# Decoder step on one core: other pacing of the mixer's convolution and LayerNorm, the last convolution tap stored to SBUF directly, sample caches read in pairs, and a different share of weights split by DMA

## Chip, core and metric

The kernel runs on one core of one Trainium2 chip. The metric is the device time of one execution in microseconds (us), from the first to the last activity of the run; less is better.

## What is computed

One inference step of a two-layer decoder over 320 tokens: 256 of a new prompt and 64 of a sample group (8 sequences of 8 tokens) that has cached state. Both groups use the same weights. Cut to what matters here, a layer is

```
x += 1/2 * SwiGLU_1(RMSNorm(x))
h  = RMSNorm(x);  u, v, q, g = split(h @ W_in)
A  = pool_mixer(u) @ w_pool * scale          # 4 groups, trailing windows 2, 4, 8, 16
z  = v_a * sigmoid(v_gate)                   # GLU
y  = causal depthwise convolution of z, 31 taps, + bias
B  = silu(LayerNorm over the 1024 channels of y) @ W_pw
C  = attention of q over 256 memory rows     # keys, values: projected (prompt) or cached (sample)
x += (sig(g_A)*A + sig(g_B)*B + sig(g_C)*C) @ W_out
x += 1/2 * SwiGLU_2(RMSNorm(x))
```

with d_model 1024, 4 heads and d_ff 2816, all in fp32. The new states, the projected keys and values and the final RMSNorm are outputs as well.

## The kernel before

Activations lie transposed: 8 blocks of 128 channels by 320 token columns. Every weight block of 128x128 fp32 numbers is split into a high part `whi` and a low part `wlo`, and each product is three matmuls of 320 columns: high by high (L309), high by low (L310), low by high (L312). A **unit** is 8 such blocks, 24 matmuls, and the text counts units from the start of the layer: the first FFN has units 0 to 65, the memory keys 66 to 73, the GLU 74 to 89, the memory values 90 to 97, q 98 to 105, the four pool groups (each with its gate g_A) to about 123, g_C to about 131, g_B to 139, then W_pw, W_out and the second FFN. Layer 1 repeats this 222 units later.

`Stream` brings the weights. Raw tiles of 1 MB (two units each, four buffers) come over SP's queue in the fixed order of `stream_plan`, which also sets where the cached keys ("k") and values ("v") of the sample group stand among them. `Stream.split` prepares a unit three units ahead of its use: ScalarE (ACT) casts the raw block to `whi` (L235) and VectorE (DVE) subtracts to get `wlo`. While `ws.share` is set, every third unit goes another way: ACT casts (L228), then writes the negative of the raw block, rounded, into `wlo` (L229), and GpSimd (POOL) issues an accumulating DMA (L230, `wlo<-in_w`) that adds the raw weights to it from HBM. There are four `whi` and four `wlo` buffers. `ws.share` is set through the whole mixer.

All arithmetic of DVE and POOL goes through a helper, so those instructions have line L127. Beside the matmuls the mixer runs small generators, stepped once per weight unit or so by `pump` at a rate that `start` gives them: `conv_gen` (rate RC) runs two lanes of the depthwise convolution, one channel block each, where ACT makes the first tap in PSUM (L503), DVE adds 30 taps there (`cv<-z,cst,cv`), and ACT copies the sum to SBUF (L510, `z<-cv`); `conv_sample` (rate RS) does the 64 sample columns on POOL (tile `pr`), and ACT adds the bias (L538). When all blocks are there, DVE sums them to `ysum`, a matmul with a matrix of ones gives the mean (L357), DVE subtracts it, ACT squares, a second such matmul gives the variance, DVE forms the reciprocal root, and after the gate "open" ACT applies silu (L585) and the cast to `chi` (L586), which W_pw multiplies. `pool_gen` (rate RP) makes the pooled inputs `plh` and `pll` from `ut`, which ACT fills from PSUM (L770). `prompt_scores` has the softmax of the prompt, with exponentials on ACT (L601). `sample_scores` and `sample_values` multiply the cached raw tiles.

Each engine runs its own queue in order. The rates only set where the program text issues a step; the order in each queue is then set by the tile framework's scheduler from its own estimate of times.

Of the kernel before, what the change touches and what calls it, by code (L numbers as in the profile page):

```python
# [17 lines left out]
TP = 256  # L18
# [14 lines left out]
LA = 3  # L33
NBIG = 8
C_LEAD = 24
RC = 2.5
RS = 1.0
RP = 2

C_G1, C_GM, C_G2, C_GK, C_PS, C_BD, C_LG, C_LB, C_WD = 0, 8, 16, 24, 32, 40, 48, 56, 64  # L40
# [11 lines left out]
def stream_plan():  # L52


    at = {}
    seq = []
    nb = 0
    for l in range(L):
        c = l * LP
        seq += list(range(c, c + MP))  # L60
        seq += list(range(c + MP + 8, c + MP + 12))
        seq += list(range(c + MP, c + MP + 8))
        seq += list(range(c + MP + 12, c + LP))
        at.setdefault((nb + NJ * 16) // 16, []).append(("m", l))
        nb += NJ * 24
        nb += 128 + 64 + 64 + 64
        for g in range(4):
            nb += 16 + (4 if g else 0)
            at.setdefault((nb + C_LEAD) // 16, []).append(("k", l, 2 * g))
            nb += 16  # L70
            at.setdefault((nb + C_LEAD) // 16, []).append(("k", l, 2 * g + 1))
        for b in range(8):
            nb += 8
            at.setdefault((nb + C_LEAD) // 16, []).append(("v", l, b))
            if b == 1:
                nb += 4
        nb += 64 + 64 + 64
        nb += NJ * 24
    assert seq and nb == 16 * len(seq) and sorted(seq) == list(range(nb // 16))
    items = []  # L80
    for n, c in enumerate(seq):
        items += at.get(n, [])
        items.append(("w", c))
    return items, seq
# [3 lines left out]
def trunk_kernel(  # L88
# [49 lines left out]
    def bigt(shape, dt, s):  # L138
        return big.tile([P] + shape, dt, name=nm(s), tag="big")
# [29 lines left out]
    def ccol(l, off, i):  # L169
        c = l * C_LAYER + off + i  # L170
        return cst[:, c:c + 1]
# [4 lines left out]
    class Stream:  # L176
# [45 lines left out]
        def split(self, u):  # L222
            c, half = seq[u // 2], u % 2
            raw = self.piece("w", c)[:, half * 1024:half * 1024 + 1024]
            hi = wp.tile([P, 1024], F32R, name=nm("whi"), tag="whi")
            lo = wp.tile([P, 1024], F32R, name=nm("wlo"), tag="wlo")
            if self.share and u % 3 == 2:
                nc.scalar.copy(hi[:, :], raw)  # L228
                nc.scalar.mul(lo[:, :], raw, -1.0)  # L229
                nc.gpsimd.dma_start(lo[:, :], w_in[c][:, half * 1024:half * 1024 + 1024], accum_op=ALU.add)  # L230
            else:
                n = 512 if u == 0 else 1024
                for e in range(0, 1024, n):
                    h, r = hi[:, e:e + n], raw[:, e:e + n]
                    nc.scalar.copy(h, r)  # L235
                    dve.tensor_tensor(out=lo[:, e:e + n], in0=r, in1=h.bitcast(F32), op=ALU.subtract)
            self.units[u] = (hi, lo)
            if half == 1:
                self.done("w", c)
# [256 lines left out]
    def conv_lane(l, z, y, blocks, zdone, cdone):  # L496

        for j in blocks:
            while j not in zdone:
                yield  # L500
            zt = z[j // 4][:, j % 4, :]
            acc = psum("cv", 2)
            nc.scalar.activation(acc[:, :TP], zt[:, 0:TP], AF.Identity, bias=ccol(l, C_BD, j), scale=ccol(l, C_WD, j))  # L503
            yield
            yield
            for k in range(1, TAPS):
                dve.scalar_tensor_tensor(out=acc[:, :TP], in0=zt[:, k:k + TP], scalar=ccol(l, C_WD, k * 8 + j),
                                               in1=acc[:, :TP], op0=ALU.mult, op1=ALU.add)
                yield
            nc.scalar.copy(y[j][:, :TP], acc[:, :TP])  # L510
            cdone.append(j)

    def conv_sample(l, z, y, zdone, cdone, sdone):

        for j in range(KB):
            while j not in zdone:
                yield
            zt = z[j // 4][:, j % 4, CB + TP:ZW]
            pr = tp.tile([P, 1280], F32, name=nm("pr"), tag="pr", bufs=1)
            pr = pr[:, :16 * TS].rearrange("p (k t) -> p k t", t=TS)  # L520
            for half in range(2):
                n = 16 - half
                v = zt[:, half * 16 * 8:half * 16 * 8 + 1]
                win = bass.AP(v.tensor, v.offset, [list(v.ap[0]), [8, n], [1, TS]])
                w = ccol(l, C_WD, (CB - 16 * half) * 8 + j)
                wv = bass.AP(w.tensor, w.offset, [list(w.ap[0]), [-8, n], [0, TS]])
                if half == 1:
                    pool.tensor_copy(pr[:, 15, :], pr[:, 0, :])
                pool.tensor_tensor(out=pr[:, 0:n, :], in0=win, in1=wv, op=ALU.mult)
                m = 8  # L530
                while m:
                    pool.tensor_tensor(out=pr[:, 0:m, :], in0=pr[:, 0:m, :], in1=pr[:, m:2 * m, :], op=ALU.add)
                    m //= 2
                yield
            yield
            while j not in cdone:
                yield
            nc.scalar.activation(y[j][:, TP:T], pr[:, 0, :], AF.Identity, bias=ccol(l, C_BD, j))  # L538
            sdone.append(j)

    def conv_gen(l, z, zdone, ch, gate):
# [35 lines left out]
            yield  # L577
        while "open" not in gate:
            yield
        ch.append((bigt([KB, T], F32R, "chi"), bigt([KB, T], F32R, "clo")))  # L580
        hi, lo = ch[0]
        for j in range(KB):
# [99 lines left out]
    def mixer(l, mh, acc, on_block):  # L682
# [13 lines left out]
                dve.tensor_tensor(out=lo[:, k, :], in0=hf[:, :], in1=hi[:, k, :].bitcast(F32), op=ALU.subtract)  # L696
                yield

        ws.share = True
        wide[0] = 0  # L700
        defer(lambda: start("norm", norm_gen(), 4), 2)
        kv_keys(l, mh)
# [3 lines left out]
        for i in range(2):  # L706
            pool.memset(z[i][:, :, 0:CB], 0.0)
            nc.gpsimd.dma_start(z[i][:, :, CB + T:ZW], sc_in[l, :, 4 * i:4 * i + 4, :])
        ch, gate, zdone = [], [], []
        for j in range(KB):  # L710
            pa = pwide() if j < 2 else pmm()
            chain(pa[:, :T], xs, T)
# [11 lines left out]
                    start("conv", conv_gen(l, z, zdone, ch, gate), RC)  # L724

            defer(zfin)
        va = bigt([2048 + KB * TS], F32, "va")
        vt = va[:, :2048].rearrange("p (b c) -> p b c", b=2)
        sgs = va[:, 2048:].rearrange("p (k t) -> p k t", k=KB)
# [5 lines left out]
        ats = qa[:, KB * TP:].rearrange("p (k t) -> p k t", k=KB)  # L735
        qz = bigt([2, 1056], F32, "qz")
        pool.memset(qz[:, :, :], 0.0)
        for o in range(KB):
            pq = pmm()
            chain(pq[:, :T], xs, T)  # L740
# [21 lines left out]
        for g in range(4):  # L762
# [43 lines left out]
            start("pool", pool_gen(), RP)  # L806
            if g % 2 == 0:
                sc = psum("sa", 1)
            sample_scores(l, qz, sc, 2 * g)
            for i in range(2):  # L810
                pg = pmm()
                chain(pg[:, :T], xs, T)
                nc.scalar.activation(merged[:, 2 * g + i, :], pg[:, :T], AF.Sigmoid)
            sample_scores(l, qz, sc, 2 * g + 1)
            drain("att")
            if g % 2 == 1:
# [2 lines left out]
                pps.append(pp)  # L819
                start("ss", sample_softmax(sc, pp), 1)  # L820

        po = None
        for o in range(KB):
            pc = pmm()
# [20 lines left out]
            if o % 4 == 0:  # L845
                drain("so")
                po = psum("sa", 1)
            sample_values(l, pps[o // 4], po, o)
            if o % 4 == 3:
                start("so", sample_out(po, ats, o // 4), 1)  # L850
        sgb = bigt([KB, T], F32, "sgb")
# [9 lines left out]
        while "conv" in side:  # L861
            for name in ("convs", "conv"):
                if name in side and next(side[name][0], "end") == "end":
                    side.pop(name, None)
        ws.share = False
        chi, clo = ch[0]
        mg = (bigt([KB, T], F32R, "mgh"), bigt([KB, T], F32R, "mgl"))
        cx = [(chi[:, k, :], clo[:, k, :]) for k in range(KB)]
# [188 lines left out]
```

## Time and profile before

| | us |
|---|---|
| runs | 1683.77, 1684.36, 1684.89 |
| median | 1684.36 |
| profiled execution, its own time | 1683.86 |
| its span, first to last instruction | 1682.1 |
| PE busy, of the span | 1640.5 (98%) |
| DVE busy | 1122.7 (67%) |
| ACT busy | 796.4 (47%) |
| POOL busy | 278.3 (17%) |
| mean granted clock of TensorE | 0.991 |

TensorE (PE) is busy nearly always, so the time is the number of matmuls plus what PE waits. The waits are read from the waits and the timeline of PE; the stages in which another engine is full are read from the windows, where a busy time near the window's length means that the engine has nothing to spare there. The units are placed in the trace by counting the weight loads.

### The profile page before, as it was taken

Reading aid. Unit: us, or ns where it says so; the run is one execution under the profiler, and the core shown is the slowest. Engines: PE = TensorE matmul, PEld = TensorE weight load, DVE = VectorE, ACT = ScalarE, POOL = GpSimd, SP = SyncE. Lnnn points to the kernel's source line nnn. Section 1 sums busy time; section 2 is a strip of 40 time slices with the busy share of each in tenths; the row PEclk is TensorE's granted clock in tenths of the full one; section 3 lists DMA queues with packets and bytes.
Section 4 is the critical chain, followed back from the end, with each engine's and each line's share of the span. In section 5 each row is a group of like instructions: output and inputs, shape, how many; then the busy total and the mean of one; then the engine's idle time right before and its main releaser. Section 6 shows DMA issues by size and latency. Waiting matters only on the chain.

```text
span 1682.1 us, 27304 instructions
## 1 busy us (share of the span) xinstructions
PE 1640.5 (98%) x11194; PEld 1590.9 (95%) x11194; DVE 1122.7 (67%) x1832; ACT 796.4 (47%) x1201; POOL 278.3 (17%) x298
## 2 busy tenths in 40 slices
PE   8999999999999999999999999999999999999996
PEld 8999999988888999999999999998988889999996
DVE  7555648999945676555465564689999367655544
ACT  5444535456645454443344443454657364444431
POOL 2000004586510000000000000047664000000000
PEclk9999999999999999999999999999999999999998
DMA  7444448786897344444444444587778954444430
GB/s 272 151 150 151 176 149 261 217 250 189 267 309 237 125 151 151 151 150 151 151 150 151 151 151 170 187 256 213 215 233 262 316 171 151 151 150 151 150 126 32
DMA packets 48189, 308.87 MB, mean 184 GB/s; under 512 B 5824, under 2 KB 5888, under 8 KB 14912
## 3 DMA queue, kind: packets, MB, share of 16 engines
q1 hardware_dynamic: 38160, 270.75, 45.1%
q0 software_dynamic: 9616, 36.05, 10.1%
q8 instruction: 88, 1.44, 0.3%
q10 hardware_dynamic: 288, 0.33, 0.1%
q14 instruction: 37, 0.30, 0.1%
HBM read 298.28 MB, written 8.82 MB: 183 GB/s over the span
## 4 chain that ended last, share of the span: by engine, by line
PE 84%; DVE 10%; POOL 2%; ACT 1%; DMA 1%; issue 1%; DVEq 0%; SPq 0%; POOLq 0%; ACTq 0%
PE mm L309 19%; PE mm L310 19%; PE mm L312 19%; PE cv L310 8%; PE cv L309 8%; PE cv L312 8%; DVE cv L127 4%; DVE wlo L127 2%; POOL pr L127 2%; DVE us L127 1%; PE sa L664 1%; DMA wlo<-in_w 1%; PE st L833 1%; DVE ysum L127 0%; DVE pll L127 0%
## 5 line engine op out<-in xcount | busy, mean ns | idle before, releaser
L235 ACT CAST whi<-raw 128x1024 fp32r<-128x1024 f32 (+1 forms) x397 | 414.8, 1045 | 438.7 <-PE mm L310 255.9
L127 DVE TENSOR_TENSOR wlo<-raw,whi 128x1024 fp32r<-128x1024 f32 (+1 forms) x397 | 502.1, 1265 | 176.9 <-PE mm L312 70.0
L309 PE MATMUL mm<-hhi,whi 128*128 128x320 f32 x1712 | 512.5, 313 | 6.6 <-ACT hhi L361 5.8
L310 PE MATMUL mm<-hlo,whi 128*128 128x320 f32 x1712 | 509.0, 311 | 0.0
L309 PEld LDWEIGHTS mm<-hhi,whi 128*128 128x128 f32 x1712 | 321.8, 188 | 18.7 <-ACT hhi L361 6.2
L310 PEld LDWEIGHTS mm<-hlo,whi 128*128 128x128 f32 x1712 | 322.1, 188 | 1.4 <-issue 0.4
L312 PE MATMUL mm<-hhi,wlo 128*128 128x320 f32 x1712 | 288.4, 309 | 0.0
L312 PEld LDWEIGHTS mm<-hhi,wlo 128*128 128x128 f32 x1712 | 260.5, 188 | 0.3
L127 DVE SCALAR_TENSOR_TENSOR cv<-z,cst,cv 128x256 f32<-128x256 f32 x480 | 204.6, 478 | 3.7 <-ACT cv L503 2.0
L230 POOL DMA_DIRECT2D wlo<-in_w x48 | 42.7, 889 | 984.2 <-ACT wlo L229 637.7
L310 PE MATMUL cv<-hlo,whi 128*128 128x320 f32 x592 | 175.4, 310 | 0.0
L309 PE MATMUL cv<-hhi,whi 128*128 128x320 f32 x592 | 174.2, 309 | 0.0
L127 POOL TENSOR_TENSOR pr<-pr 128x512 f32<-128x512 f32 (+3 forms) x128 | 124.6, 973 | 7.7
L309 PE MATMUL mm<-hidh,whi 128*128 128x320 f32 x418 | 123.8, 309 | 0.0
L310 PE MATMUL mm<-hidl,whi 128*128 128x320 f32 x418 | 123.7, 309 | 0.0
L365 ACT CAST hidh<-up 128x320 fp32r<-128x320 f32 x88 | 40.0, 459 | 159.5 <-DVE up L127 159.5
L310 PEld LDWEIGHTS cv<-hlo,whi 128*128 128x128 f32 x592 | 111.2, 188 | 0.2
L309 PEld LDWEIGHTS cv<-hhi,whi 128*128 128x128 f32 x592 | 110.9, 188 | 0.0
L312 PE MATMUL cv<-hhi,wlo 128*128 128x320 f32 x592 | 98.8, 309 | 0.0
L312 PEld LDWEIGHTS cv<-hhi,wlo 128*128 128x128 f32 x592 | 89.9, 188 | 0.2
L127 DVE TENSOR_TENSOR up<-mm,rstd 128x320 f32<-128x320 f32 x53 | 26.0, 490 | 88.2 <-PE mm L312 88.2
L309 PE MATMUL cv<-hidh,whi 128*128 128x320 f32 x286 | 84.7, 309 | 0.0
(196 smaller groups left out, 2324.7 us busy)
## 6 DMA issues: line engine op xcount, KB each, us to landing
raw<-in_w SPq DMA_DIRECT2D x221, 1024.0 KB, 4.8
wlo<-in_w POOLq DMA_DIRECT2D x48, 512.0 KB, 7.8
raw<-in_kc SPq DMA_DIRECT2D x16, 1024.0 KB, 7.5
raw<-in_vc SPq DMA_DIRECT2D x16, 1024.0 KB, 7.5
out_co<-z POOLq DMA_DIRECT2D x16, 135.0 KB, 5.1
raw<-in_mem SPq DMA_DIRECT2D x2, 1024.0 KB, 4.8
out_mk<-kt POOLq DMA_DIRECT2D x2, 1024.0 KB, 10.2
out_mv<-va POOLq DMA_DIRECT2D x2, 1024.0 KB, 5.2
```

Of the source, the lines that this page charges most:

```text
L127: return op(*args, **kw)
L230: nc.gpsimd.dma_start(lo[:, :], w_in[c][:, half * 1024:half * 1024 + 1024], accum_op=ALU.add)
L235: nc.scalar.copy(h, r)
L309: nc.tensor.matmul(out, hi, xh, start=(i + e == 0), stop=False)
L310: nc.tensor.matmul(out, hi, xl, start=False, stop=False)
L312: nc.tensor.matmul(out, lo, xh, start=False, stop=(i + e == last))
L365: nc.scalar.copy(hi, src)
L664: nc.tensor.matmul(po[32 * h:32 * h + 32, :256], pp[:, at:at + 32], raw[:, mb * 1024 + h * 256:mb * 1024 + h * 256 + 256], start=(bb == 0 ...
L833: nc.tensor.matmul(pv[:, :TP], vt[:, mb, o * P:o * P + P], kt[:, 2 * hd + mb, :], start=(mb == 0), stop=(mb == 1))
```

## The change

- Pacing: RC goes from 2.5 to 3, RS from 1 to 2 with two more stopping points in each block's work, and once the gate is open the rate of the convolution's generator, which by then does the last part of LayerNorm, is set to a new RN of 6.
- The first convolution tap moves from ACT to DVE (a `tensor_scalar` into PSUM); the last of the 30 additions writes the SBUF tile itself, so that ACT's copy L510 is gone.
- The sample caches are read in pairs: both key tiles of a group behind its two g_A blocks, before one ahead of them and one behind; value tiles two at every second g_C block. `stream_plan` places the tiles accordingly.
- `ws.share` takes every second unit, not every third, but is set only in the GLU stage and from q to the end of the pool groups of each layer: four stages in all. Since a split runs three units ahead, these are units 78 to 92 and 102 to 126 of a layer.

The counts of instructions that differ: the accumulating DMAs and ACT's negations 48 to 42, DVE's subtractions `wlo` 395 to 401; ACT's first taps and copies 16 and 16 to none; DVE gets 16 `tensor_scalar`; ACT's table loads 26 to 30. The number of matmuls is the same.

```diff
@@ constants
-RC = 2.5
-RS = 1.0
+RC = 3.0
+RN = 6.0
+RS = 2.0
@@ stream_plan
         for g in range(4):
-            nb += 16 + (4 if g else 0)
-            at.setdefault((nb + C_LEAD) // 16, []).append(("k", l, 2 * g))
-            nb += 16
-            at.setdefault((nb + C_LEAD) // 16, []).append(("k", l, 2 * g + 1))
-        for b in range(8):
-            nb += 8
-            at.setdefault((nb + C_LEAD) // 16, []).append(("v", l, b))
-            if b == 1:
-                nb += 4
+            nb += 32 + (4 if g else 0)
+            at.setdefault((nb + C_LEAD) // 16, []).extend([("k", l, 2 * g), ("k", l, 2 * g + 1)])
+        for b in range(1, 8, 2):
+            nb += 16 + (4 if b == 1 else 0)
+            at.setdefault((nb + C_LEAD) // 16, []).extend([("v", l, b - 1), ("v", l, b)])
@@ Stream.split
-            if self.share and u % 3 == 2:
+            if self.share and u % 2 == 0:
@@ conv_lane
-            nc.scalar.activation(acc[:, :TP], zt[:, 0:TP], AF.Identity, bias=ccol(l, C_BD, j), scale=ccol(l, C_WD, j))
-            yield
+            dve.tensor_scalar(out=acc[:, :TP], in0=zt[:, 0:TP], scalar1=ccol(l, C_WD, j), scalar2=ccol(l, C_BD, j),
+                              op0=ALU.mult, op1=ALU.add)
             yield
             for k in range(1, TAPS):
-                dve.scalar_tensor_tensor(out=acc[:, :TP], in0=zt[:, k:k + TP], scalar=ccol(l, C_WD, k * 8 + j),
+                dst = acc[:, :TP] if k < TAPS - 1 else y[j][:, :TP]
+                dve.scalar_tensor_tensor(out=dst, in0=zt[:, k:k + TP], scalar=ccol(l, C_WD, k * 8 + j),
                                                in1=acc[:, :TP], op0=ALU.mult, op1=ALU.add)
                 yield
-            nc.scalar.copy(y[j][:, :TP], acc[:, :TP])
             cdone.append(j)
@@ conv_sample
                 pool.tensor_tensor(out=pr[:, 0:n, :], in0=win, in1=wv, op=ALU.mult)
+                yield
                 m = 8
                 while m:
                     pool.tensor_tensor(out=pr[:, 0:m, :], in0=pr[:, 0:m, :], in1=pr[:, m:2 * m, :], op=ALU.add)
                     m //= 2
+                    if m == 4:
+                        yield
                 yield
@@ conv_gen
         while "open" not in gate:
             yield
+        side["conv"][1] = RN
@@ mixer
-        ws.share = True
         kv_keys(l, mh)
...
+        ws.share = True
         for j in range(KB):          # GLU
...
+        ws.share = False
         kv_values(l, mh, vt)
...
+        ws.share = True
         for o in range(KB):          # q
...
-            sample_scores(l, qz, sc, 2 * g)
             for i in range(2):
                 pg = pmm()
                 chain(pg[:, :T], xs, T)
                 nc.scalar.activation(merged[:, 2 * g + i, :], pg[:, :T], AF.Sigmoid)
+            sample_scores(l, qz, sc, 2 * g)
             sample_scores(l, qz, sc, 2 * g + 1)
...
+        ws.share = False
         for o in range(KB):          # g_C
...
-            sample_values(l, pps[o // 4], po, o)
+            if o % 2 == 1:
+                sample_values(l, pps[o // 4], po, o - 1)
+                sample_values(l, pps[o // 4], po, o)
...
-        ws.share = False
         chi, clo = ch[0]
```

The queues' order changes in three places that the prediction speaks of. The first is PE's queue around the matmul that gives LayerNorm's mean (`ysum`, the sum of the eight blocks; `hhi` and `hlo` are the normalised input, `mm`, `cv` and `st` PSUM tiles). Before, in layer 0, it stands behind unit 133, in the g_B stage:

```order
L309 MATMUL mm_5323<-hhi_2483,whi_5185 128x320
L310 MATMUL mm_5323<-hlo_2484,whi_5185 128x320
L312 MATMUL mm_5323<-hhi_2483,wlo_5186 128x320 x8
L357 MATMUL cv_5377<-ysum_2809,ones 128x320
L309 MATMUL mm_5361<-hhi_2483,whi_5236 128x320
```

In the changed kernel it stands inside unit 125, in g_C's first blocks (`st<-kt,va` is attention of the prompt):

```order
L306 MATMUL mm_4935<-hhi_2483,whi_4760 128x320
L307 MATMUL mm_4935<-hlo_2484,whi_4760 128x320
L354 MATMUL cv_4815<-ysum_2807,ones 128x320
...
L309 MATMUL mm_4935<-hhi_2483,wlo_4761 128x320 x4
L837 MATMUL st_4978<-kt,va_3351 128x256 x2
```

It moved ahead by eight units of weights, and the variance's matmul, which follows it, stands in unit 127 and no longer in 137. In layer 1 the mean's matmul stands one unit earlier still, in 124 by the same count. W_pw begins at unit 140 in both.

The second is ACT's queue in pool group 1 of layer 0, between the copy of the transposed scores `kt` and the copies to `ut`. Before:

```order
L229 ACTIVATE wlo_4086<-raw_3872 128x1024
L630 COPY kt<-st_4075 128x512
L510 COPY z_2732<-cv_3920 128x256
L235 CAST whi_4127<-raw_3978 128x1024
L601 ACT_TABLE_LOAD
L601 ACTIVATE ex_4137,sm_4139<-st_4096,mx_4138 128x256 x2
L503 ACTIVATE cv_4622<-z_2732,cst 128x256
L770 COPY ut_4081<-mm_4084 128x320
```

Changed:

```order
L804 CAST plh_4027<-us_4032 128x640
L815 ACTIVATE merged_3908<-mm_4062 128x320
L538 ACTIVATE z_2730<-pr_3711,cst 128x64
L631 COPY kt<-st_4125 128x512
L225 CAST whi_4178<-raw_4011 128x1024
L602 ACT_TABLE_LOAD
L602 ACTIVATE ex_4189,sm_4191<-st_4147,mx_4190 128x256 x2
L773 COPY ut_4131<-mm_4134 128x320
L226 ACTIVATE wlo_4179<-raw_4011 128x1024
```

The copy `z<-cv`, which waits for DVE's taps, and the first tap `cv<-z,cst` are gone from between them; the accumulated exponentials now follow a cast and a table load directly, and a negation `wlo<-raw` stands behind the first copy to `ut`.

The third is POOL's queue around the last sample block of the convolution in layer 0. Before:

```order
L127 TENSOR_TENSOR pr_5020<-z_2732,cst 128x1024
...
L127 COPY pr_5020<-pr_5020 128x64
L127 TENSOR_TENSOR pr_5020<-z_2732,cst 128x960
L771 DMA out_po<-ut_4564 128x2x135
L127 TENSOR_TENSOR pr_5020<-pr_5020 128x512
L127 TENSOR_TENSOR pr_5020<-pr_5020 128x256
L127 TENSOR_TENSOR pr_5020<-pr_5020 128x128
L127 TENSOR_TENSOR pr_5020<-pr_5020 128x64
L230 DMA wlo_4722<-in_w 128x1024
L127 MEMSET ut_12289 128x2x15
L765 DMA ut_12289<-in_sp 128x2x120
L127 MEMSET qz_3540 128x1056
```

Changed:

```order
L124 COPY pr_4511<-pr_4511 128x64
L124 TENSOR_TENSOR pr_4511<-z_2730,cst 128x960
L124 TENSOR_TENSOR pr_4511<-pr_4511 128x512
L124 MEMSET ut_12328 128x2x15
L768 DMA ut_12328<-in_sp 128x2x120
L124 TENSOR_TENSOR pr_4511<-pr_4511 128x256
L227 DMA wlo_4803<-in_w 128x1024
L124 TENSOR_TENSOR pr_4511<-pr_4511 128x128
L124 MEMSET qz_3572 128x1056
L124 TENSOR_TENSOR pr_4511<-pr_4511 128x64
```

The fill of `ut`, the load of its sample columns, one accumulating DMA and the fill of `qz` stood behind the block's last addition and now stand among its additions, ahead of the last one.

## Rows read from the trace of the kernel before

**Rows 1.** The page, part 1: busy us, share of the span, instructions.

```profile
PE 1640.5 (98%) x11194; PEld 1590.9 (95%) x11194; DVE 1122.7 (67%) x1832; ACT 796.4 (47%) x1201; POOL 278.3 (17%) x298
```

**Rows 2.** The page, part 4: the chain that ended last, by engine.

```profile
PE 84%; DVE 10%; POOL 2%; ACT 1%; DMA 1%; issue 1%; DVEq 0%; SPq 0%; POOLq 0%; ACTq 0%
```

**Rows 3.** Windows of the mixer: us, engines' busy us (instructions), granted clock, DMA share, GB/s.

```profile
310.00:350.00 40.00, 36.99 (x203) 33.08 (x203) 39.58 (x71) 20.55 (x27) 31.30 (x30) 1.00 0.76 211
350.00:395.00 45.00, 45.00 (x309) 43.78 (x308) 44.08 (x84) 30.14 (x62) 31.62 (x30) 1.00 0.77 223
395.00:450.00 55.00, 51.57 (x363) 44.63 (x362) 53.95 (x107) 32.44 (x55) 29.00 (x34) 0.97 0.76 246
...
1225.00:1280.00 55.00, 51.66 (x364) 44.70 (x363) 53.95 (x107) 32.96 (x56) 28.16 (x33) 0.97 0.75 243
```

**Rows 4.** Waits of PE: engine line waited for, us in total, times, longest us.

```profile
PE mm L309 <- ACT chi L586: 7.9, 2, 3.9
PE mm L309 <- ACT ut L770: 7.3, 5, 3.0
PE mm L490 <- DMA wlo<-in_w: 6.3, 2, 3.2
```

**Rows 5.** Windows, five short stretches, columns as above.

```profile
411.56:414.97 3.41, 3.41 (x16) 1.88 (x16) 3.41 (x5) 2.10 (x5) 3.21 (x2) 0.50 0.00 0
548.10:554.90 6.80, 6.20 (x23) 6.20 (x24) 3.97 (x9) 5.79 (x14) 0.00 (x0) 0.50 0.47 157
1172.73:1176.14 3.41, 3.41 (x10) 2.64 (x9) 3.22 (x7) 0.00 (x0) 1.51 (x3) 0.50 0.78 191
1241.00:1244.40 3.40, 3.40 (x18) 1.78 (x17) 3.40 (x5) 1.69 (x4) 3.32 (x3) 0.50 0.00 0
1377.53:1380.94 3.41, 3.41 (x14) 3.41 (x14) 1.49 (x4) 3.41 (x9) 0.00 (x0) 0.50 0.67 279
```

**Rows 6.** Timeline of PE: start us, us, instruction; inside unit 125, mean's matmul.

```profile
476.46 0.31 PE L309 MATMUL mm<-hhi,whi 128*128 128x320 f32 x1
...
522.41 0.70 PE L357 MATMUL cv<-ysum,ones 128*128 128x320 f32 x2
```

**Rows 7.** Timeline of ACT, layer 0: a copy and what follows it.

```profile
406.90 0.38 ACT L510 COPY z<-cv 128x256 f32<-128x256 f32 x1 [5.01 <-DVE cv L127]
...
408.24 1.28 ACT L601 ACT_TABLE_LOAD   x1
...
410.94 0.43 ACT L770 COPY ut<-mm 128x320 f32<-128x320 f32 x1
```

**Rows 8.** Timeline of POOL, layer 0: the issue for the unit that PE waits for.

```profile
337.19 0.89 POOL L230 DMA_DIRECT2D wlo<-in_w  x1 [0.18 <-issue]
```

**Rows 9.** One line (L230) of 270 to 560: DMA landings.

```profile
DMA to landing us min/median/max: 5.2/7.9/11.3
```

**Rows 10.** Groups by line, 279 to 459: busy us, mean ns, idle before.

```profile
L127 DVE SCALAR_TENSOR_TENSOR cv<-z,cst,cv 128x256 f32<-128x256 f32 x240 | 102.2, 477 | 1.9 <-ACT cv L503 1.0
...
L127 DVE TENSOR_TENSOR wlo<-raw,whi 128x1024 fp32r<-128x1024 f32 x30 | 46.5, 1549 | 0.5 <-PE mm L312 0.3
...
L229 ACT ACTIVATE wlo<-raw 128x1024 fp32r<-128x1024 f32 x15 | 15.9, 1060 | 0.1
...
L503 ACT ACTIVATE cv<-z,cst 128x256 f32<-128x256 f32 x8 | 4.5, 568 | 2.7 <-DVE z L127 2.6
...
L510 ACT COPY z<-cv 128x256 f32<-128x256 f32 x8 | 3.0, 372 | 7.6 <-DVE cv L127 7.5
```

**Rows 11.** Timeline of POOL, layer 0: the last sample block.

```profile
450.44 1.97 POOL L127 TENSOR_TENSOR pr<-z,cst 128x1024 f32<-128x1024 f32 x1
...
464.26 0.92 POOL L230 DMA_DIRECT2D wlo<-in_w  x1
...
469.21 1.00 POOL L127 MEMSET qz<- 128x1056 f32 x1
```

**Rows 12.** Timeline of DVE, layer 0: the last addition to ysum.

```profile
466.60 0.49 DVE L127 TENSOR_TENSOR ysum<-ysum,z 128x320 f32<-128x320 f32 x1
```


## The prediction

> **What bounds the kernel now.** I read the page's engine shares first, then the chain, then the windows over the mixer, then PE's waits. PE is busy 1640.5 of 1682.1 us [rows 1] and holds 84% of the chain that ended last; DVE holds 10% of it [rows 2]. So a microsecond is gained only where PE stands still or runs at half clock, or where matmuls go, and no matmul goes here. The windows show a second limit: from 310 to 450 us, the stretch with the depthwise convolution, DVE is busy 39.58 of 40, 44.08 of 45 and 53.95 of 55 us, and in layer 1 again 53.95 of 55 [rows 3]. DVE is full there while PE still has a little idle time. A PE wait in that stretch can only be handed back as far as DVE keeps up.
>
> PE's waits that the change touches come in three kinds, each once per layer [rows 4]: for `chi`, LayerNorm's last product (7.9 us together); for the copy to `ut` (7.3 us in five waits, of which two long ones of about 3.0); and for an accumulating DMA in the memory values (6.3 us). Five stretches of half clock (0.50, the 1.2 GHz level) follow waits of some 3 to 4 us [rows 5]: one after each `chi` wait, one after each `ut` wait, one after the DMA wait of layer 1. They cost half their length where PE had work: 3.1 us of the stretch at 548.10 (6.20 busy), 1.7 of each 3.41.
>
> **The change, part by part.**
>
> *LayerNorm earlier.* The mean's matmul ran at 522.41 us and would now stand in unit 125, a place that PE passed at 476.46 [rows 6]; the variance follows two units behind and not four. In the new order the last casts of `chi` stand in unit 134, six units ahead of W_pw, and a unit lasts 24 x 0.147 = 3.5 us, so there are some 20 us of cover. Even 10 us of lateness leaves `chi` in time. The two waits go with their half clock: 7.9 + 3.1 + 1.7 = **12.7 us** [rows 4, 5].
>
> *Unit 95 is no longer shared.* Its DMA was issued only at 337.19 [rows 8], because POOL stood in the sample block. DVE now makes this `wlo`. The two waits go, with layer 1's half clock: 6.3 + 1.7 = **8.0 us** [rows 4, 5]. Units 90 and 92 remain shared; unit 92's place in PE's queue is the same as before, so I cost it at nothing, covered by the landing that was in time before.
>
> *ACT's copies go.* At 406.90 ACT had waited 5.01 us for DVE's taps in order to copy them; the table load, exponentials and the copy to `ut` at 410.94 stood behind it [rows 7], and PE waited for `ut`. In the new queue nothing of the taps stands there. Two waits of 3.0 with two half-clock stretches: 6.0 + 3.4 = **9.4 us** [rows 4, 5]. Next in line there is DVE (the pooled inputs). The four additional table loads take 1.28 us each, like the one from 408.24 to 409.53 [rows 7]; ACT is busy 20.55 of 40 and 32.44 of 55 us [rows 3], so its idle time hides them.
>
> If nothing came back, that would be 12.7 + 8.0 + 9.4 = 30.1 us.
>
> *What DVE must do.* Between the last z (330 us) and the last tap, by my count of the queue, DVE has 26 subtractions where it had 29, and eight first taps more. Three subtractions at 46.5/30 = 1.55 us are 4.6 us less. The first tap as a `tensor_scalar` into PSUM has no row: below it is bounded by a later tap, 102.2/240 = 0.43 us, above by ACT's 0.57 for the same work [rows 10]; I take 0.43, the same engine and shape, and get 3.4 us more (at most 4.6). So DVE's load is about 1 us smaller per layer (0 to 2): **practically unchanged**. The last tap's store to SBUF I cost at nothing, below at nothing and above at 0.1 us each, as its neighbours are of equal length; 16 are 1.6 us. DVE therefore cannot finish the taps 8 us earlier, though PE could. The generous pacing also changes the mixture: in the new queue more taps of the first six blocks stand behind subtractions and pooled sums, and block 6 ends, by adding the rows' durations along the queue, some 4 us later than before.
>
> *LayerNorm's first wait.* The mean needs `ysum`, whose last addition ran at 466.60 [rows 12], after POOL's last block, which took from 450.44 to 464.26 [rows 11], 13.8 us. In the new queue an accumulating DMA's issue (0.92), the fill of `qz` (1.00) and the fill and load of `ut` (I take 0.9 for both, as for the other issue) stand inside that block [rows 11]: 2.8 us more. With block 6 later by 4, `ysum` is done near 466.6 + 0.5 + 2.8 + 4 = 474 us of the old time scale. PE would be there at 476.46 less the 3.2 of unit 95 and 4.7 of `ut`, at about 468.6. In a queue in order it waits: about 5 us. Layer 1 has the mean's matmul one unit earlier but had 1.7 us more to give; I take 5 there too. **Given back: 10 us** of the 17.4; from 2 (DVE and POOL overlap better than added up) to 17.4 (all of it).
>
> *New sharing in the GLU stage.* Every second unit now needs an accumulating DMA. For most of them PE has 14.1 us of matmuls between the release of the buffer and the need (96 of 0.147), and the path is a cast of 1.05, a negation of 1.06 [rows 10], 0.3 to the issue and 7.9 to landing [rows 9], 10.3 in sum: covered, and the slowest landing of 11.3 still is, nearly. Unit 78 has only 53 matmuls, 7.8 us, since units 74 to 77 run interleaved. It is late by 2.5 us at the median landing; by 0 at the fastest (5.2) and 5.9 at the slowest. I take 2.2, as PE has small delays there too: **4.4 us more** for both layers, range 0 to 12.
>
> The Trainium skill, page "DMA: Bandwidth & Descriptors", section "Anatomy of one DMA", fits a GpSimd-issued DMA by 2.0 us plus its bytes at 436 GB/s, which for 512 KB would be an estimate of 3.2 us. By that rule unit 78 would be in time and the sum 4.4 us lower. The trace does not agree: of 22 landings none was under 5.2 us [rows 9].
>
> *Caches in pairs.* The same 32 tiles and matmuls in another order; they land ahead of use by several us before. Nothing, with an upper bound of 1 us per pair at four value pairs of each layer: 0 to 8. The six fewer accumulating DMAs lie in stages that were not late, apart from unit 95.
>
> **Sum**: -12.7 - 8.0 - 9.4 + 10 + 4.4 = -15.7 us. The profiled execution took 1683.86 us, 1.8 more than its span and 0.5 less than the median of the runs; from it, 1668.2: I forecast **1668 us**. Own range: 1660 (2 given back, unit 78 in time) to 1676 (nearly all given back).
>
> **The rivals.**
> *All waits vanish (B).* DVE's queue and POOL's fit after all and the DMAs land: 1683.9 - 30.1 = 1654. For it: DVE loses its dependence on ACT at both ends of a block, with 5.0 us waits of ACT on it. Against: DVE is 98% busy [rows 3]. Chance 0.12.
> *Only `chi` remains (D).* DVE and POOL give back everything ahead of the mean, and the GLU waits stay: 1683.9 - 12.7 + 4.4 = 1676. For it: the full windows [rows 3]. Chance 0.20.
> *The mean waits too long (C, slower).* The mean's and variance's matmuls stand in PE's queue in front of g_C's weights, which have nothing to do with LayerNorm. Each us that `ysum` or the squares come after PE stops all matmuls behind. The place is units 125 and 127; the price is 1 us per us, plus 1.7 of half clock. It decides from the point where the waits in both layers eat 30.1 - 4.4 = 25.7 us: 12.8 us per layer, `ysum` at about 481 and not 474. With 16 us per layer the time is 1683.9 - 30.1 + 4.4 + 32 = 1690. Against: POOL's block is only 2.8 us longer by the rows. For it: in the old order 55 us lay between `ysum` and its use [rows 6, 12], and now none. Chance 0.08; that it just cancels the gain (1681.0 to 1687.7), 0.07.
> *The page's rule (P).* Landing after 3.2 us at unit 78: 1664. Chance 0.03 beside the rows.
>
> **How the numbers follow.** Forecast 0.50, B 0.12, D 0.20, C 0.08, just cancelled 0.07, P 0.03. About 0.2% (3.4 us) is what a measurement of this kernel can tell from no change. Faster by more: 0.50 + 0.12 + 0.20 + 0.03 = 0.85; within: 0.07; slower: 0.08. The range takes in the forecast, D, P and most of B with their uncertainties: 1653 to 1681, leaving out the cancelled and slower cases and a little below.
>
> **What would show it.** In the profile after: no wait of PE for `chi`, and no half clock near W_pw's start; no wait for `wlo` in the memory values; no wait for `ut`; a new PE wait for DVE's `ysum` in front of the mean's matmul, 3 to 7 us in each layer; a PE wait of 1 to 4 us for `wlo<-in_w` at the start of the GLU; DVE still above 95% busy from 310 to 450. It is wrong if PE's waits at the mean are absent (then B) or above 12 us (then C), or if `chi` still is waited for.

## The result and the profile after

The changed kernel took 1659.72 us in the median of four runs (1659.35 to 1660.38), against 1684.07 for the kernel before (1683.05 to 1684.89): a ratio of 0.9856, 95% interval 0.9839 to 0.9873, 24.4 us less. 1668 was forecast, with a range of 1653 to 1681. The profiled execution took 1659.87, its span is 1657.9 us, 24.2 less than before.

The page of the changed kernel, part 1, the chain's first line, and the landing times (part 6):

```profile
PE 1630.5 (98%) x11194; PEld 1585.8 (96%) x11194; DVE 1120.4 (68%) x1854; ACT 784.0 (47%) x1167; POOL 266.7 (16%) x292
...
PE 86%; DVE 7%; issue 3%; DMA 3%; ACT 1%; POOL 0%; DVEq 0%; SPq 0%; ACTq 0%; POOLq 0%
...
wlo<-in_w POOLq DMA_DIRECT2D x42, 512.0 KB, 7.1
```

The number of matmuls is the same and PE's busy time fell by only 10 us: the five stretches of half clock [rows 5] held 19.8 us of matmuls before, and at full clock these take half of that. PE's waits (engine line waited for, us in total, times, longest):

```profile
PE mm L306 <- ACT hhi L358: 5.8, 1, 5.8
PE sa L640 <- DMA raw<-in_kc: 2.8, 3, 1.7
PE mm L309 <- DMA wlo<-in_w: 2.3, 3, 1.4
PE mm L306 <- ACT ut L773: 2.1, 3, 1.0
```

The wait for `chi` is gone, that for `ut` fell from 7.3 to 2.1 us, that of the memory values is gone [rows 4]. Two new ones came: for cached key tiles, 2.8, and for accumulating DMAs, 2.3, of which 1.7 at the GLU's start and 0.7 in pool group 1 of layer 0. The wait for `hhi` is the program's start, 5.8 us in both kernels.

The windows over the mixer, with W_pw's start as the last (columns as in [rows 3]):

```profile
310.00:350.00 40.00, 40.00 (x223) 36.23 (x222) 39.03 (x72) 20.01 (x25) 30.78 (x29) 1.00 0.70 205
350.00:395.00 45.00, 45.00 (x323) 43.64 (x323) 43.98 (x94) 28.33 (x56) 28.48 (x31) 1.00 0.84 243
395.00:450.00 55.00, 53.62 (x380) 47.99 (x382) 55.00 (x114) 37.93 (x65) 33.41 (x38) 1.00 0.94 280
1210.00:1265.00 55.00, 52.96 (x371) 47.40 (x370) 54.97 (x114) 37.82 (x65) 32.74 (x35) 1.00 0.93 278
535.00:560.00 25.00, 25.00 (x173) 25.00 (x172) 15.80 (x24) 9.58 (x13) 0.00 (x0) 1.00 0.39 140
```

The half clock is gone from the mixer; one stretch is left in both kernels, the last 8.6 us of the program (11.0 before). The mean over the span is 0.997 where it was 0.991. DVE is still full: 55.00 of 55 us from 395 to 450. What it got done in that time is where the forecast went wrong, so the groups of DVE from the first z to the last tap of layer 0 stand here, the window moved to the changed kernel's times (columns as in [rows 10]):

```profile
L124 DVE SCALAR_TENSOR_TENSOR cv<-z,cst,cv 128x256 f32<-128x256 f32 x232 | 97.2, 476 | 0.1
L124 DVE TENSOR_TENSOR wlo<-raw,whi 128x1024 fp32r<-128x1024 f32 x26 | 36.1, 1388 | 2.2 <-ACT whi L232 2.2
...
L124 DVE TENSOR_SCALAR cv<-z,cst 128x256 f32<-128x256 f32 x8 | 4.3, 537 | 0.1
L124 DVE SCALAR_TENSOR_TENSOR z<-z,cst,cv 128x256 f32<-128x256 f32 x8 | 3.8, 470 | 0.0
...
L124 DVE TENSOR_TENSOR pll<-us,plh 128x640 fp32r<-128x640 f32 x3 | 2.4, 810 | 0.0
```

The subtractions `wlo` and the taps before are in [rows 10]; `pll` before:

```profile
L127 DVE TENSOR_TENSOR pll<-us,plh 128x640 fp32r<-128x640 f32 x3 | 6.7, 2234 | 0.0
```

### The profile page after: what moved, and what is told of

Its sections match the earlier page's. It is cut to its first block, busy times and chain, and to the rows that moved or that the text cites. A ratio compares the mean times of both kernels' runs of the same rounds, so it can differ in the third digit from the quotient of the medians.

```text
span 1657.9 us, 27271 instructions
## 1 busy us (share of the span) xinstructions
PE 1630.5 (98%) x11194; PEld 1585.8 (96%) x11194; DVE 1120.4 (68%) x1854; ACT 784.0 (47%) x1167; POOL 266.7 (16%) x292
## 4 chain that ended last, share of the span: by engine, by line
PE 86%; DVE 7%; issue 3%; DMA 3%; ACT 1%; POOL 0%; DVEq 0%; SPq 0%; ACTq 0%; POOLq 0%
PE mm L306 19%; PE mm L309 19%; PE mm L307 19%; PE cv L309 8%; PE cv L306 8%; PE cv L307 8%; DVE cv L124 3%; DMA raw<-in_kc 2%; DVE us L124 1%; DVE wlo L124 1%; PE sa L665 1%; PE mm L484 1%; PE mm L483 1%; PE mm L487 1%; PE st L837 1%
## 5 line engine op out<-in xcount | busy, mean ns | idle before, releaser
L232 ACT CAST whi<-raw 128x1024 fp32r<-128x1024 f32 (+1 forms) x403 | 420.6, 1045 | 428.3 <-PE mm L307 252.9
L307 PE MATMUL mm<-hlo,whi 128*128 128x320 f32 x1712 | 507.8, 310 | 0.0
L124 DVE SCALAR_TENSOR_TENSOR cv<-z,cst,cv 128x256 f32<-128x256 f32 x464 | 194.6, 476 | 0.2
```

Of the source, the lines that this page charges most:

```text
L124: return op(*args, **kw)
L307: nc.tensor.matmul(out, hi, xl, start=False, stop=False)
```

## The experiments

All ratios are to the kernel before on the same chip in the same session; a percent is 16.8 us. First each part was undone alone in the changed kernel, then each was made alone in the kernel before.

**Old pacing.** The rates, the two stopping points and RN as before, all else changed:

```diff
-RC = 3.0
-RN = 6.0
-RS = 2.0
+RC = 2.5
+RS = 1.0
@@ conv_sample: both new yields taken out
@@ conv_gen
-        side["conv"][1] = RN
```

> The changed kernel with the old pacing of convolution, sample block and LayerNorm (no other part undone). In its queues the mean's matmul stands in unit 131 and the last chi casts behind unit 140, W_pw's first. Theory (the pacing alone moves LayerNorm, worth the two chi waits with their half clock): both chi waits come back, 12 to 13 us more than the changed kernel, about 1672. Rival (LayerNorm became early because DVE finished the taps 8 us earlier, thanks to the first and last tap and the sharing): chi waits of under 1 us each, about 1660 to 1662.

Measured: 1675.27 us, ratio 0.9950 (0.9935 to 0.9965), 15.8 us worse than the changed kernel's ratio. PE's waits and the windows around W_pw's start in both layers:

```profile
PE mm L305 <- ACT chi L582: 4.9, 4, 2.2
...
PE mm L305 <- ACT sgb L856: 2.4, 2, 1.2
```

```profile
535.00:560.00 25.00, 21.18 (x120) 19.46 (x120) 12.77 (x22) 16.86 (x26) 0.00 (x0) 0.86 0.25 88
1358.00:1382.00 24.00, 20.33 (x105) 18.46 (x104) 10.38 (x19) 15.06 (x24) 0.00 (x0) 0.79 0.17 62
```

The chi waits are back, 4.9 us and 2.4 for `sgb`, the gate g_B, beside them; at a granted clock of 0.86 over 25 us and 0.79 over 24, half clock took up to 3.5 + 5.0 us more. That adds up to 15.8 at most, some idle time being counted in both. DVE's taps end at 451.3 us here too, with `ysum` begun for the last time at 468.7 as in the changed kernel (468.6). So early taps alone do not bring LayerNorm forward: the mean's matmul stands in unit 131 and runs at 507.8, 39 us after its input. The theory holds in its sign and its place, with 3 us more than it put; the rival falls. The pacing is several settings (RC, RS with the stopping points, RN), and which of them brings LayerNorm forward was not separated.

**Old taps.** First tap and last copy on ACT again:

```diff
-            dve.tensor_scalar(out=acc[:, :TP], ...)
+            nc.scalar.activation(acc[:, :TP], zt[:, 0:TP], AF.Identity, ...)
...
+            nc.scalar.copy(y[j][:, :TP], acc[:, :TP])
```

> The changed kernel with the first tap and the last copy back on ACT. Theory (ACT's copy, which waits for DVE's taps, delayed the copy to ut): two ut waits of about 3 us with half clock come back, 6 to 9 us more, about 1666 to 1669. Rival (the wait went because DVE's queue runs earlier there, whatever ACT does): within 2 us of the changed kernel's 1659.7.

Measured: 1669.96 us, ratio 0.9918 (0.9899 to 0.9937), 10.4 us worse. PE's waits:

```profile
PE mm L306 <- ACT ut L773: 5.1, 4, 1.7
PE mm L309 <- DMA wlo<-in_w: 4.6, 4, 3.4
PE st L630 <- ACT ex L607: 3.8, 2, 2.4
```

The waits for `ut` grew from 2.1 to 5.1 us, but these were not two waits of 3; there are more and shorter ones, also for the softmax (3.8) and for accumulating DMAs (4.6). The size was a little above the expected 6 to 9, the place right only in part. The taps of layer 0 now end at 463.8, not 451.2.

**Old share.** Every third unit, through the whole mixer:

```diff
-            if self.share and u % 2 == 0:
+            if self.share and u % 3 == 2:
@@ mixer: ws.share set once at its start, cleared ahead of W_pw
```

> The changed kernel with every third unit shared through the whole mixer, as before. Theory (unit 95 and its DMA, issued late behind POOL's block, were the cause of the wait in the memory values): waits of about 3 us for wlo<-in_w return in both layers, with half clock in one or both, 6 to 10 us more, less the 2 us that the wait at the start of the GLU costs the changed kernel: 1664 to 1668. Rival (POOL's other pacing already issues that DMA in time): 1657 to 1660.

Measured: 1669.23 us, ratio 0.9912 (0.9897 to 0.9927), 9.4 us worse.

```profile
PE mm L306 <- ACT ut L771: 5.2, 5, 1.3
PE mm L309 <- DMA wlo<-in_w: 3.2, 3, 1.6
PE mm L487 <- DMA wlo<-in_w: 2.7, 2, 1.5
PE mm L306 <- DVE merged L124: 2.4, 2, 1.2
```

The wait of the memory values is back, but with 2.7 us over the two layers and no half clock it is a part of the 9.4 only. The rest are waits for `ut` (5.2) and DVE (2.4). The taps end at 460.8. The theory's size was a little low, and its place was one of several.

**Caches one by one.** `stream_plan`, `sample_scores` and `sample_values` as before:

```diff
-            if o % 2 == 1:
-                sample_values(l, pps[o // 4], po, o - 1)
-                sample_values(l, pps[o // 4], po, o)
+            sample_values(l, pps[o // 4], po, o)
@@ and the first sample_scores of a group ahead of the g_A blocks again
```

> The changed kernel with the cached tiles one by one, as before. Theory (the pairs are worth nothing, and PE's wait for raw<-in_kc of 2.8 us comes with them): 1657 to 1660, no wait for raw<-in_kc. Rival (the pairs keep the value tiles or the transposes out of PE's way): 2 us or more slower than 1659.7.

Measured: 1671.07 us, ratio 0.9925 (0.9903 to 0.9947), 11.6 us worse; its runs spread over 6.6 us. The theory fell: the pairs, costed at nothing, matter in the changed kernel. In the profiled execution, the shortest of the four, PE waited 6.4 us for `ut` (longest 4.1) and 3.8 for POOL's `qz`. Undone one kind at a time:

> The changed kernel with the key tiles one by one, the value tiles in pairs. Theory (undoing the pairs cost 11 us because a key tile's matmuls ahead of the g_A blocks bring PE to the next product earlier and move the row maximum in DVE's queue, so that ut is late): waits for ut come back, 1665 to 1672. Rival (the values are the cause): 1658 to 1662.

> The changed kernel with the value tiles one by one, the key tiles in pairs. Theory (the keys matter, the values do not): 1658 to 1662. Rival (single value tiles and the wait for POOL's qz belong together): waits for qz of 1 to 3 us, 1663 or more.

Measured: keys 1665.63 us, ratio 0.9895 (0.9876 to 0.9913); values 1665.06, ratio 0.9895 (0.9880 to 0.9910); each 6.6 us worse. For the keys the theory's waits for `ut` are there:

```profile
PE mm L308 <- ACT ut L775: 9.2, 2, 5.1
```

For the values it fell, and the rival's numbers came: 1665, with a wait for `qz` of 1.2 us in one layer. That wait is the smaller part. The profiled execution took 3.9 us longer than the changed kernel's, of which 1.3 are waits for `qz`; 2.8 are in the 256 matmuls of the sample values themselves, which kept PE busy for 18.9 us and not 16.1. Why they take longer is not shown. With the keys undone, ACT's queue in layer 0 shows how `ut` becomes late:

```profile
405.41 1.28 ACT L604 ACT_TABLE_LOAD   x1 [7.70 <-DVE mx L126]
406.71 0.47 ACT L604 ACTIVATE ex<-st,mx 128x256 f32<-128x256 f32 x1
...
408.57 0.42 ACT L775 COPY ut<-mm 128x320 f32<-128x320 f32 x1
```

ACT waited 7.70 us for the row maximum `mx`, and the copy to `ut` stood behind the exponentials. The maximum was late for two reasons, as DVE's and POOL's timelines show:

```profile
402.28 0.68 DVE L126 TENSOR_REDUCE mx<-st 128x2 f32<-128x512 f32 x1
...
403.66 1.67 DVE L126 TENSOR_SCALAR mx<-mx 128x2 f32<-128x2 f32 x1
```

```profile
403.48 1.83 POOL L126 TENSOR_TENSOR pr<-z,cst 128x960 f32<-128x960 f32 x1
```

In the changed kernel the reduction came at 400.75, 1.5 us earlier in DVE's full queue:

```profile
400.75 0.68 DVE L124 TENSOR_REDUCE mx<-st 128x2 f32<-128x512 f32 x1
...
402.13 0.46 DVE L124 TENSOR_SCALAR mx<-mx 128x2 f32<-128x2 f32 x1
```

And the scaling of two numbers per partition, 0.46 us there, took 1.67 here: it ended at 405.33, when POOL's product, from 403.48 with 1.83 us, ended at 405.31. Besides, the changed kernel loads the table at 399.96, while it waits, and here the load came after the wait. So the copy L510 was only one of the ways in which DVE's lateness reached `ut`.

**Pacing alone.**

```diff
-RC = 2.5
-RS = 1.0
+RC = 3.0
+RN = 6.0
+RS = 2.0
@@ conv_sample, conv_gen as in the change; all else as before
```

> The kernel before with the new pacing alone. In its queues the mean's matmul stands in unit 123, the variance's in 126, the last chi casts in 134. Theory (pacing alone is worth the chi waits, and the waits in the memory values and for ut stay): 12 to 13 us less than before, about 1671. Rival (without the other parts DVE is late and PE waits at the mean's matmul for ysum): less than 8 us gained, a PE wait for ysum above 2 us in each layer.

Measured: 1670.41 us, ratio 0.9923 (0.9908 to 0.9938): 13.0 us gained.

```profile
PE mm L310 <- ACT ut L775: 6.0, 2, 3.0
...
PE mm L491 <- DMA wlo<-in_w: 5.3, 2, 2.8
```

No wait for `chi`, none of 0.5 us or more for `ysum`; the two others stay nearly whole (7.3 and 6.3 before). The theory holds to within half a microsecond.

**Taps alone.** (`conv_lane` as in the change.)

> The kernel before with the first and last tap changed alone. Theory (ACT's copy was the one cause of the ut wait): the two ut waits go, 6 to 9 us less than before, about 1676; the chi waits stay or shrink a little (mean's matmul in unit 131). Rival (the exponentials' wait for DVE's row maximum, which stand ahead of the copy to ut in ACT's queue, is a second cause): ut waits of 1 to 4 us remain, 0 to 4 us gained.

Measured: 1671.14 us, ratio 0.9930 (0.9914 to 0.9947): 11.8 us gained, more than expected.

```profile
PE mm L309 <- ACT chi L586: 2.9, 4, 0.9
PE mm L490 <- DMA wlo<-in_w: 2.8, 2, 1.4
PE mm L309 <- ACT sgb L855: 2.7, 2, 1.3
PE mm L309 <- ACT ut L770: 0.8, 1, 0.8
```

The wait for `ut` is nearly gone, as the theory says; but the taps also end 4 us earlier here (454.8), so this run alone does not tell ACT's copy from DVE's time. The others shrank as well: that of the memory values from 6.3 to 2.8, and LayerNorm's from 7.9 to 5.6 (`chi` and `sgb`), its mean standing in unit 131 instead of 133.

**Share alone.** (`Stream.split` and the four stages as in the change.)

> The kernel before with the new share of accumulating DMAs alone. Theory: the waits of the memory values go (6 to 8 us less), the GLU's start costs 2 us: 1677 to 1680. Rival (DVE, which makes three more subtractions in the FFN's end, is later for it and the ut wait grows): 1682 or more.

Measured: 1688.28 us, ratio 1.0030 (1.0019 to 1.0041): 5 us slower.

```profile
PE mm L309 <- ACT chi L586: 6.8, 2, 3.4
...
PE mm L309 <- ACT ut L772: 5.0, 3, 3.0
PE mm L312 <- DMA wlo<-in_w: 4.5, 5, 2.3
PE sa L664 <- issue: 3.3, 2, 1.7
PE st L651 <- ACT exs L606: 2.2, 2, 1.1
PE mm L310 <- DVE clo L127: 1.8, 2, 0.9
```

The wait of the memory values is gone, but accumulating DMAs are late elsewhere (4.5 us), and small waits came for sample values, softmax and `clo`. The rival had the sign, not the mechanism: the wait for `ut` did not grow. The theory was right about the wait that goes and wrong about the time.

**Caches alone.** (`stream_plan` and the two loops as in the change.)

> The kernel before with the cached tiles in pairs alone. Theory (a wait goes only when all its causes go, and with ACT's copy still in its queue the pairs change nothing): 1683 to 1686, ut waits as before. Rival (the pairs alone shorten the wait for ut, as undoing them cost 11 us in the changed kernel): 5 us or more gained.

Measured: 1683.94 us, ratio 1.0001 (0.9992 to 1.0011). The theory holds: nothing.

Made alone, the parts give -13.0, -11.8, +5 and 0, together -20; undone alone they cost 15.8, 10.4, 9.4 and 11.6, together 47; all four give 24.4. By their intervals the first four are good to 2 or 3 us, the others, differences of two ratios, to 4 or 5. They are not additive: share and caches gain nothing alone, and cost when they are undone with the other parts there.

**POOL's sums left out**, in the kernel before:

```diff
                 while m:
-                    pool.tensor_tensor(out=pr[:, 0:m, :], in0=pr[:, 0:m, :], in1=pr[:, m:2 * m, :], op=ALU.add)
                     m //= 2
```

> The kernel before without POOL's additions of the sample convolution (it leaves out the sums over the taps of the 64 sample columns; the products stay). It tells what DVE and the accumulating DMA lose to POOL. Theory (DVE's operations with two SBUF inputs are held up by POOL's, and that decides how late the taps end): the subtractions between 279 and 459 us fall from 1.55 us in the mean to below 1.35, the taps end 6 us or more earlier, and the waits in the memory values (POOL's issue is early now) and for ut both shrink: 8 us or more gained. Rival (POOL does not hold DVE up, the long subtractions have another cause): the mean stays near 1.55, only the memory values' waits go, 3 to 8 us gained.

Measured: 1673.0 us, ratio 0.9940 (0.9925 to 0.9955): 10 us gained. The subtractions in the same window:

```profile
L127 DVE TENSOR_TENSOR wlo<-raw,whi 128x1024 fp32r<-128x1024 f32 x30 | 40.2, 1342 | 2.6 <-ACT whi L235 1.7 <-PE mm L312 0.3
...
L127 DVE TENSOR_TENSOR pll<-us,plh 128x640 fp32r<-128x640 f32 x3 | 3.4, 1119 | 0.0
```

They fell from 1.55 to 1.34 us, `pll` from 2.23 to 1.12; the taps ended at 453.5 and not 458.8, 5.3 us earlier (6 expected); the wait in the memory values fell from 6.3 to 1.7, that for `ut` from 7.3 to 5.1. The theory holds, somewhat smaller than put: POOL's sums hold DVE up. The traces show it one by one as well, if the subtractions are sorted by whether arithmetic of POOL ran at the same time. In the kernel before 20 of the 30 ran beside it and took 1718 ns in the mean, the ten others 1210 (at most 1216). With the sums left out only 8 ran beside POOL's products, 1687 ns, and 22 did not, 1216. The taps, which read one tensor from SBUF and one from PSUM, show nothing of it: 478 ns beside POOL and 475 without it in the kernel before.

**The two remaining waits.**

```diff
-        ws.share = True
         for j in range(KB):          # GLU
+            if j == 1:
+                ws.share = True
@@ stream_plan
-            ....extend([("k", l, 2 * g), ("k", l, 2 * g + 1)])
+            at.setdefault((nb + C_LEAD - 16) // 16, []).append(("k", l, 2 * g))
+            at.setdefault((nb + C_LEAD) // 16, []).append(("k", l, 2 * g + 1))
```

> The changed kernel with sharing set one GLU block later (units 78 and 300 of the two layers are subtracted by DVE) and the first key tile of each pair sent for one weight tile earlier. Theory (the changed kernel's remaining waits for wlo<-in_w at the GLU's start, 2 us, and for raw<-in_kc, 2.8 us, are what is left there): 1655 to 1658. Rival (the order that the scheduler makes for the whole mixer shifts and other waits of DVE's full queue take their place): 1660 to 1672.

Measured: 1658.67 us, ratio 0.9856 (0.9841 to 0.9870), the same ratio as the changed kernel's, so the theory falls.

```profile
PE mm L307 <- ACT ut L775: 5.7, 6, 1.3
...
PE mm L310 <- DMA wlo<-in_w: 0.2, 1, 0.2
```

The two waits are gone (0.2 us and none), but the waits for `ut` rose from 2.1 to 5.7. What was taken out in one place came back in another, as the rival says, while DVE is full.

## Why the prediction was right, and where it was off

The sign and the range held. The forecast missed 8 us of the gain: the 10 us that it gave back at the mean's matmul did not come. The step that failed stands before that, in what DVE must do.

*LayerNorm earlier*: right. Forecast 12.7 us, measured 13.0 with the pacing alone. In the changed kernel the mean's matmul runs at 469.13 and the casts of `chi` begin at 514.49, with W_pw's first matmul at 537.2.

*Unit 95*: right in place, the wait is gone. But the share has no price of 8.0 us of its own: made alone it loses 5, undone it costs 9.4, of which 2.7 are that wait.

*ACT's copies go*: the wait went to 2.1 us, and the taps alone leave 0.8. The size was right and the account of the cause too narrow: with the copies gone, undoing the key pairs alone brings 9.2 us of waits for `ut` back, through the softmax. The taps alone also shortened the waits of LayerNorm and of the memory values, which I had not counted.

*What DVE must do*: **this step failed**. It said that DVE's load is practically unchanged, about 1 us less, that DVE cannot finish the taps 8 us earlier, and that the sixth block ends 4 us later. Measured in layer 0 from the first z to the last tap: 279.1 to 458.8 before, 283.3 to 451.2 after, 179.7 us against 167.9; 180.6 and 169.1 in layer 1. DVE's busy time between these points fell from 175.9 to 164.4 us, the last tap came 7.6 us earlier, and the sixth block was done at 403.8 and not 407.3, 3.5 us earlier. The count was right (26 subtractions that begin between the two points where 29 did, 8 first taps more) and the first tap's price nearly so (0.45 us from start to start, 0.43 taken). But the durations that I used came from operations that POOL had held up, and I took them as if they belonged to the operation. The subtractions fell from 1549 to 1388 ns, which is 4.2 us over 26: 17 ran beside POOL, with 1481 ns in the mean where it had been 1718, and 9 did not, with 1213. `pll` fell from 2234 to 810 ns, 4.3 us over three (in layer 1 from 1324 to 811, 1.5 us). With the three subtractions fewer (4.6) and the first taps (3.6 more) that makes 9.5 of the 11.8 us.

POOL's sums are still all there, so what changed is how long they and DVE's operations met; the orders of both queues differ, and no run shows which difference did it. POOL's pacing is not what avoided the collisions: with the old one the taps take 167.8 us. Old taps (180.6) or old share (181.6) each undo all of it in layer 0, and taps alone (175.8) or share alone (174.8) give 4 to 5. A part of the rest is the start: where the new share meets ACT's first tap, that tap stands behind ACT's casts, and DVE's first addition comes 4.3 us after the first z and not 1.2. Counted from that first addition, the taps take 178.5 us before, 174.6 with the taps alone, 170.5 with the share alone and 166.6 in the changed kernel with the old pacing: 3.9 and 8.0 add up to its 11.9. What is not settled is why each is worth less than alone when the new pacing and the pairs stand beside it and the other part does not (old taps 176.2, old share 180.4).

*LayerNorm's first wait*: 10 us given back were forecast, 0.3 and none came. PE came when forecast (468.7 and 468.6, in part by luck, since new waits lie ahead of it), but `ysum` was done at 469.1 and not 474:

```profile
450.74 0.48 DVE L124 SCALAR_TENSOR_TENSOR z<-z,cst,cv 128x256 f32<-128x256 f32 x1
```

```profile
466.23 0.60 POOL L124 TENSOR_TENSOR pr<-pr 128x64 f32<-128x64 f32 x1
```

POOL's last block took 5.5 us longer and not 2.8 (447.5 to 466.8), but began 3 us earlier, when ACT's bias for the block before it was done, and so ended 2.5 us later, about as forecast. From its end to the sum it took 2.2 us, before 2.8. The 4 us that the forecast added for DVE's sixth block are what did not come: DVE's last tap was done at 451.2, 15.6 us before the end of POOL's block, and was not what `ysum` waited for. The matmul stands four matmuls into unit 125, and PE came there just as its input did:

```profile
468.74 0.31 PE L307 MATMUL mm<-hlo,whi 128*128 128x320 f32 x1
469.13 0.81 PE L354 MATMUL cv<-ysum,ones 128*128 128x320 f32 x2
```

In every kernel with the new pacing the mean's matmul ran within 4 us behind `ysum` and PE waited 0.5 us or less for it at a time. That fits a scheduler that puts it where its own estimate has the input ready; the estimate itself is not in the record. A faster DVE is not needed for it: with the pacing alone the taps take 178.2 us, and PE, with the matmul two units further ahead and its other waits still there, came at 467.6, just behind `ysum` (466.3). With the old taps `ysum` was done at 473.3, nearly the 474 of the forecast, and the kernel took 1670, near the 1668; but PE had lost that time in waits for `ut`, the softmax and accumulating DMAs, and at the mean it waited for nothing. I had carried the old time scale to the new order and set a full engine's delay against it.

*Sharing in the GLU*: right place, less than half the size. PE waited 0.2 us for unit 78 in layer 0, where its DMA landed after 5.4 us, and 1.4 in layer 1, after 6.6; 4.4 were forecast for both, with a landing of 7.9.

*The page's rule*: the landings of the changed kernel from 270 to 560 us were 5.2 to 11.1, 7.5 in the median, so the estimate of 3.2 us by the fit in the Trainium skill, page "DMA: Bandwidth & Descriptors", section "Anatomy of one DMA", is again below all of them.

*Caches in pairs*: nothing alone, as costed, but with the rest their undoing costs 11.6 us; as a term of the sum the price depends on which of the others is there. The wait for key tiles, 2.8 us, lies within the bound of 8.

*The range and the rivals*: the own range of 1660 to 1676 has a slip. With 2 us given back and unit 78 in time the sum is 1655.8; 1660 is what it gives with the 4.4 us of unit 78 still in it. The measured 1659.7 lies between the two, at the end where nearly nothing is given back. The rival "all waits vanish" (1654), with a chance of 0.12, came nearest in mechanism, and the prediction's own sign for it, no wait at the mean, is what the trace shows; what kept it from being right are the new waits for key tiles and accumulating DMAs, 5.1 us, and the remaining 2.1 for `ut`: 1653.8 + 7.2 = 1661.0, against 1659.87 in the profiled execution.

## What to carry to other kernels

Where an engine is full and its neighbour slows it, do not price its work by the mean of durations that contain collisions: sort them by whether the neighbour ran at the same time, and take the two means as the two ends. When two queues are near their limit, a wait has several sufficient causes, so undoing one part and making one part alone give different prices, and both are needed. A matmul that waits for a side chain may be moved ahead without loss if the order puts it where its input arrives: here the pacing that did so was worth 13 us alone.

## What the runs showed of the hardware

An operation of two numbers per partition can cost 1.5 us on a path that matters: the scaling of `mx` took 1.67 us while POOL's product ran and ended with it; over the program the eight of them took 264 ns in the mean before, 488 after and 164 with POOL's sums left out. The Trainium skill, page "SBUF — State Buffer", section "Who interferes with whom", says that DVE and GpSimd share a pair of ports as an exclusive lock, which one of the two then holds for a whole instruction, that a `tensor_scalar` from SBUF to SBUF can take it under conditions, and that an operation with two SBUF inputs contends with GpSimd's reads. The runs agree: 1.67 us beside the 1.83 of POOL's product, and subtractions of 1718 ns beside POOL's work and 1210 without it.

The first tap, one input and two scalars per partition, takes 0.45 us from start to start into PSUM, more than a later tap with two inputs at 0.39; and the last tap's store to SBUF instead of PSUM changes nothing (470 against 476 ns for the taps before it).
